# Relative-position bias rows of a fused transformer: written to a small HBM scratch and copied from there, instead of copied out of eight partitions

## The chip, the cores and the metric

One core of one Trainium2 chip runs the whole program in one launch. The metric is the device time of one execution in microseconds (us); the time before is the median of 3 runs. Instruction times in the profile are counted from the first instruction of the program; this length is called the span.

## The reference

Two layers of a first block (feed-forward, a mixer with three attention branches, feed-forward) are followed by one layer of a second block, whose attention adds a learned bias by relative position. Sequence 512, width 1024, feed-forward width 2816, float32. What the change touches is the bias:

```python
def dilated_group_attention(q, k, v, bias_tab, window, dilation):
    ...
    offset = a - c + n_prev * BLOCK
    bias = bias_tab[rel_bucket(offset * dilation)].astype(jnp.float32).transpose(2, 0, 1)
    ...
    s = jnp.einsum('brnqhd,brnkhd->brnhqk', qb, kb).astype(jnp.float32) * (Dh ** -0.5) + bias
    s = jnp.where(valid[:, None], s, NEG_INF)

def swiglu_ffn(x, g, w_gu, w_down):
    h = rms_norm(x, g)
    gate, up = jnp.split(h @ w_gu, 2, axis=-1)
    return (jax.nn.silu(gate) * up) @ w_down
```

The bias depends on the difference of two positions alone, so one row of 384 values per head (3 groups of 8 heads) holds all of it. Query i reads its own window of that row, shifted by one place from query to query.

## The kernel before

Every product is computed as three float32r matmuls (lines 172 to 174), high times high, high times low, low times high, with 128x128 of weights as the stationary side and 512 tokens as the moving side. The weights come as one stream of 550 units of 128x1024 float32 (512 KB). `w_dma` (line 133) loads unit u on the SP queue into one of three staging slots. `w_prep` (lines 141, 142) turns it into a high and a low half with one ScalarE copy and one VectorE subtraction, in a ring of five units, up to three units ahead of the one in use. A load is issued when the subtraction has freed its staging slot. One unit feeds 8 x 3 = 24 matmuls.

The program starts with the first feed-forward, `gen_ffn`. It walks over 22 chunks of 128 hidden channels: 16 weight tiles (48 matmuls) for gate and up, then `evac` (lines 261 to 263, 179, 180). Chunks 0 and 1 go together; behind them the norm's statistics are summed (line 218), turned into a reciprocal root on VectorE (lines 205 to 223) and spread over the partitions (lines 231, 232). Program order is priority: a scheduler orders each engine's instructions from it and from its own simulated times.

`bias_rows` is called once from this feed-forward. For each of the three groups it multiplies the table by one-hot rows (line 1015, in PSUM), adds the mask (line 1018, 8 partitions x 384), and issues one DMA on the GpSimd queue that writes each of the 8 rows 128 times into `dr_b` in HBM, 1.5 MB (line 1019):

```python
            if cs[0] == 2 and self.first:
                self.first = False
                self.bias_rows()
...
            nc.gpsimd.dma_start(self.dr_b[g], t[:, None, :].to_broadcast([8, 128, 384]))
```

`dr_b` is read far later, in the second block: `load_bias` reads it with a step of 383 instead of 384 from partition to partition, which gives each query its shifted window.

Of the kernel before, what the change touches and what calls it, by code (L numbers as in the profile page):

```python
# [19 lines left out]
NEG = -1.0e30  # L20
# [73 lines left out]
def const_r():  # L94
    """Stationaries: -1 where row >= column; -1 all over; identity; the strict-past mask."""
    c = np.zeros((128, 512), np.float32)
    p = np.arange(128)
    c[:, 0:128] = np.where(p[:, None] >= p[None, :], -1.0, 0.0)
    c[:, 128:256] = -1.0
    c[:, 256:384] = np.eye(128)  # L100
    c[:, 384:512] = np.where(p[:, None] < p[None, :], 0.0, NEG)
    return c
# [7 lines left out]
class Build:  # L110
# [65 lines left out]
    def split(self, hi, lo, src, scale=None):  # L176
        """hi + lo = src * scale, to float32's precision."""
        if scale is None:
            self.nc.scalar.activation(hi, src, AF.Copy)  # L179
            self.nc.vector.tensor_tensor(lo, src, hi, op=ALU.subtract)  # L180
        else:
            self.nc.scalar.activation(hi, src, AF.Copy, scale=scale)
            self.nc.vector.scalar_tensor_tensor(lo, src, scale, hi, op0=ALU.mult, op1=ALU.subtract)  # L183
# [28 lines left out]
    def stats_a(self, accs, ps, eps=1e-6, ts=range(4)):  # L212
        """Column sums of the accs into token-major rstd [128, 4]."""
        nc = self.nc
        first = None
        for i, acc in enumerate(accs):
            for t in ts:
                first = self.behind(first, nc.tensor.matmul(
                    ps[:, t:t + 1], lhsT=acc[:, 128 * t:128 * t + 128], rhs=self.f(A_C + C_ONE, 1), start=first is None,
                    stop=i == len(accs) - 1, skip_group_check=True))  # L220
        sm = self.f(A_SM, 16)
        v, a, b, y = (sm[:, i + ts[0]:i + ts[-1] + 1] for i in (4, 8, 12, 0))
        nc.vector.tensor_scalar(v, ps[:, ts[0]:ts[-1] + 1], 1.0 / D, eps, op0=ALU.mult, op1=ALU.add)
        self.rsqrt(y, v, a, b)
        return y

    def bcast(self, cols, dg, ps, out):
        """out[:, t*128 + i] = cols[i, t] on every partition."""
        nc = self.nc
        for t in range(cols.shape[-1]):  # L230
            nc.vector.tensor_scalar_mul(dg[:, 128 * t:128 * t + 128], self.f(A_C + C_ID, 128), cols[:, t:t + 1])
        nc.tensor.matmul(ps, lhsT=self.f(A_C + C_ONE, 128), rhs=dg, start=True, stop=True)
        nc.scalar.activation(out, ps, AF.Copy)
# [10 lines left out]
    def gen_ffn(self, wgu, wdn, l, done, halves=None):  # L244
# [22 lines left out]
        def up(cs):  # L267
            ps = {(c, up): self.bank(ring) for c in cs for up in (0, 1)}
            order = [(c, up, k) for c in cs for up in (0, 1) for k in range(8)]
            if len(cs) == 2:  # L270
                order.sort(key=lambda e: e[2])
            for c, up, k in order:
                self.mm3(ps[c, up], self.w(gkey(c, up, k)), self.h(k), k == 0, k == 7)
                yield
            if len(cs) == 2:
                pst = self.bank(ring)
                self.bcast(self.stats_a((self.acc,), pst), tt_flat, pst, rb)
            for c in cs:
                evac(c, ps[c, 0], ps[c, 1])
            if cs[0] == 2 and self.first:  # L280
                self.first = False
                self.bias_rows()
# [3 lines left out]
        def down(grp, cs):  # L286
# [17 lines left out]
            # the last channels a half of the tokens at a time  # L304
# [22 lines left out]
    def ffn_add(self, gain, last=None):  # L327
        """x += 0.5 * rstd * product; the second half also readies the next operand."""
        nc = self.nc

        def done(grp, m, ps, t, rb):
            x = self.x(m)
            nc.vector.tensor_tensor(t, ps, rb, op=ALU.mult)
            nc.vector.scalar_tensor_tensor(x, t, 0.5, x, op0=ALU.mult, op1=ALU.add)
            if grp == 1:
                if gain is None:
                    nc.gpsimd.dma_start(self.ap["out"][:, m, :], x)
                else:
                    self.x_done(m, gain)
        return done  # L340

    def drive(self, main, side=None):
        """Program order is priority: the side stream goes first, the main one as far as it is waited for."""
        alive = True

        def step():
            nonlocal alive
            try:
                next(main)
            except StopIteration:  # L350
                alive = False

        if side is not None:
            for tok in side:
                if isinstance(tok, str):
                    while tok not in self.flags:
                        assert alive, tok
                        step()
        while alive:
            step()  # L360

    def behind(self, first, ins):
        """A product issues behind the one that opens its bank (the first, when there is none yet)."""
# [7 lines left out]
    @contextlib.contextmanager  # L371
    def late(self, by):
        """Work that other work goes before where both are ready."""
        tc = self.tc
        p = tc.cur_priority
        tc.cur_priority = max(0, p + by)
        yield
        tc.cur_priority = p
# [7 lines left out]
    def gen_mix(self, l):  # L386
# [69 lines left out]
        # compressed branch: the rows (parity, channel) of its first product's operand  # L456
# [69 lines left out]
        # the first branch's part of the merge, in the operand's place  # L526
# [14 lines left out]
    def merged(self, m):  # L541
        """Where the merge of a chunk of channels gathers."""
        return self.mt[:, 512 * m:512 * m + 512]

    def h_tile(self, dtype=F32R):
        """The products' operand; while none is there, the merge's sums."""
        return self.hp.tile([128, 8192 if dtype == F32R else 4096], dtype, name="h", tag="h")

# [1 line left out]
    def rope(self, x, co, si, h, tmp):  # L550
        """x: [128, b, n, >= 2h], co/si: [128, b, 2h]."""
# [12 lines left out]
    def norm_heads(self, x, nh, gain, sq, sm):  # L564
        """x: [128, nh, 64] in place: rms norm over the last axis, times gain."""
# [15 lines left out]
    def one_gain(g):  # L581
        """The same gain for every head."""
# [5 lines left out]
    def tpose_dup(self, ps, src, tmp, rep=2):  # L588
        """src [128 tokens, n, d]: each [tokens, d] transposed into a column block, rep times down the partitions."""
# [8 lines left out]
    def gen_idx(self, l):  # L598
# [62 lines left out]
        # the key of the sparse branch  # L661
# [7 lines left out]
        # gates of the three branches  # L669
# [44 lines left out]
    def sb_pair(self, hp):  # L714
        """Two heads of the stick-breaking branch, key blocks from the last to the first."""
# [44 lines left out]
    def attn_pair(self, q, k, mask, n, gate, v, out, first):  # L760
        """Two heads over n keys: out[channel, token] += gated softmax times values, a head in each half of the rows."""
# [43 lines left out]
    def q2_prep(self, b, src, nh):  # L805
        """Transposed [hi; lo] queries of one block of tokens: [128, nh * 128]."""
# [28 lines left out]
    def q_prep(self, o, nh, g, sm):  # L835
        """Queries of 4 * nh heads at o: norm and rotation in place."""
# [5 lines left out]
    def gen_nsa(self, l):  # L842
# [8 lines left out]
        def prep(b):  # L851
            """Queries, and the compressed branch's numerators, transposed."""
# [152 lines left out]
    def bias_rows(self):  # L1005
        """Relative-position bias rows of every head, to DRAM."""
# [6 lines left out]
        for g in range(3):  # L1013
# [5 lines left out]
            nc.gpsimd.dma_start(self.dr_b[g], t[:, None, :].to_broadcast([8, 128, 384]))  # L1019
# [95 lines left out]
    def conv(self, c, u):  # L1115
        """Causal depthwise filter of one chunk of channels, a tap at a time in the background."""
# [26 lines left out]
    def gen_attn2(self):  # L1143
# [30 lines left out]
        def tok(g):  # L1174
            """The statistics in DRAM, [token, group, kind, head], as group g's layout has the tokens."""
# [5 lines left out]
        for hp in range(4):  # L1181
# [25 lines left out]
            # statistics of the three groups meet token by token  # L1207
# [94 lines left out]
    def gen_ln(self):  # L1302
        """Layer norm over channels of the filtered signal, silu, split for the product."""
# [34 lines left out]
    def post(self, y, next_gain, rb, ts=range(4), pool=()):  # L1338
        """x += rms_norm(y) * gain, y transposed with the gain already in it, its squares summed."""
# [85 lines left out]
    def run(self, upto=99, start=0):  # L1425
        tc, nc, ap = self.tc, self.nc, self.ap
        with tc.tile_pool(name="sb", bufs=1) as sb, tc.tile_pool(name="hp", bufs=1) as self.hp, \
# [11 lines left out]
            self.dr_b = dr.tile([3, 8, 128, 384], F32, name="dr_b")  # L1439
            self.dr_c = dr.tile([8, 128, 512], F32, name="dr_c")  # L1440
# [63 lines left out]
def tile_t(v):  # L1504
    """[..., 1024] -> [128, 8] per vector, side by side."""
# [4 lines left out]
def par_array(inp):  # L1510
    """Small parameters, one [128, PAR] array per phase."""
# [25 lines left out]
def bias_consts():  # L1537
    """Rows of one-hot buckets by position, 383 or 255 long, and what is added: 0, or NEG where no key is."""
# [46 lines left out]
```

## Time and profile before

| | |
|---|---|
| median of 3 runs | 3584.28 us |
| lowest, highest | 3582.41, 3585.07 us |
| span of the profiled execution | 3581.1 us |
| PE busy in it | 3481.8 us, 97% |
| weight stream, SP queue | 290.49 MB, 24.1% of 16 DMA engines |
| GpSimd queue | 61.76 MB, 6.8% of 16 DMA engines |

The execution that was profiled has no other time of its own than its span; the runs' median lies 3.2 us above it, and what lies around the span is taken as that. The profile names engines PE (TensorE matmul), DVE (VectorE), ACT (ScalarE), POOL (GpSimd) and SP (its DMA queue). PEclk is the share of TensorE's full clock that was granted. DMA queue q1 carries the weight stream, q0 what GpSimd issues.

### The profile page before, as it was taken

To read this page: it belongs to the slowest core of one execution; us is meant where nothing else is said; L and a number is where in the kernel's file an instruction comes from. 1 tells how busy PE (TensorE), PEld (TensorE's weight loads), DVE (VectorE), ACT (ScalarE), POOL (GpSimd) and SP (SyncE) were. 2 spreads that over 40 slices of the span, in tenths; PEclk is the share of its full clock that TensorE was granted. 3 is DMA by queue.
4 is the path that set the end of the run, shared out by engine and by line. 5 is a ranking of instruction groups with operands and counts; after the bars stand their busy time and mean duration, and the time that the engine had idled before them with its cause. 6 is when DMAs were issued, how large, how long until landed. Compare 5 with 4: busy or idle time off the path is not lost.

```text
span 3581.1 us, 43236 instructions
## 1 busy us (share of the span) xinstructions
PE 3481.8 (97%) x16884; PEld 2802.7 (78%) x16884; DVE 2001.0 (56%) x3733; ACT 1316.6 (37%) x2234; POOL 320.8 (9%) x355
## 2 busy tenths in 40 slices
PE   7899999999999999999999999999999999999997
PEld 5688888776788888888787768888877777878886
DVE  4243488566543344434876666433488988544334
ACT  3222354356332233223544464222334443443222
POOL 2000100011300010001000104000111112210002
PEclk9899999999999999999999999999999999999999
DMA  6722332331322222223322314222332224522221
GB/s 148 116 94 94 119 94 86 103 114 62 121 90 98 94 97 89 99 94 112 95 89 101 114 38 147 94 94 94 114 100 86 81 78 142 182 77 94 95 94 54
DMA packets 100814, 357.05 MB, mean 100 GB/s; under 512 B 14168, under 2 KB 16984, under 8 KB 99808
## 3 DMA queue, kind: packets, MB, share of 16 engines
q1 hardware_dynamic: 81504, 290.49, 24.1%
q0 software_dynamic: 18144, 61.76, 6.8%
q8 instruction: 132, 2.16, 0.2%
q10 hardware_dynamic: 960, 2.04, 0.2%
q14 instruction: 74, 0.61, 0.1%
HBM read 320.05 MB, written 32.08 MB: 98 GB/s over the span
## 4 chain that ended last, share of the span: by engine, by line
PE 90%; issue 3%; DMA 3%; DVE 2%; ACT 1%; POOL 1%; another core or an unknown queue 0%; DVEq 0%; ACTq 0%; POOLq 0%
PE pb L172 27%; PE pb L173 27%; PE pb L174 27%; DMA af<-wst 2%; PE pb L801 1%; PE pb L777 1%; PE pb L793 1%; PE pb L1193 1%; PE pb L737 1%; PE pb L1290 1%; PE pb L1266 1%; PE pb L595 0%; PE pb L756 0%; DMA af<-x 0%; PE pb L751 0%
## 5 line engine op out<-in xcount | busy, mean ns | idle before, releaser
L172 PE MATMUL pb<-h,ar 128*128 128x512 f32 x2848 | 1132.8, 401 | 34.6 <-ACT ar L141 16.4
L141 ACT ACTIVATE ar<-af 128x1024 fp32r<-128x1024 f32 x550 | 582.5, 1059 | 1565.1 <-PE pb L173 993.2
L174 PE MATMUL pb<-h,ar 128*128 128x512 f32 x2848 | 1140.7, 401 | 0.1
L173 PE MATMUL pb<-h,ar 128*128 128x512 f32 x2848 | 1140.1, 400 | 0.0
L142 DVE TENSOR_TENSOR ar<-af,ar 128x1024 fp32r<-128x1024 f32 x550 | 687.2, 1250 | 448.6 <-ACT ar L141 435.6
L172 PEld LDWEIGHTS pb<-h,ar 128*128 128x128 f32 x2848 | 540.8, 190 | 167.3 <-ACT ar L141 17.3
L174 PEld LDWEIGHTS pb<-h,ar 128*128 128x128 f32 x2848 | 540.6, 190 | 130.4 <-issue 3.2
L173 PEld LDWEIGHTS pb<-h,ar 128*128 128x128 f32 x2848 | 540.7, 190 | 129.0 <-issue 3.2
L173 PE MATMUL pb<-ar 128*128 128x512 f32 (+1 forms) x1254 | 484.0, 386 | 1.2 <-DVE ar L183 1.2
L174 PE MATMUL pb<-ar 128*128 128x512 f32 (+1 forms) x1254 | 483.3, 386 | 0.0
L172 PE MATMUL pb<-ar 128*128 128x512 f32 (+1 forms) x1254 | 482.4, 387 | 0.6 <-DVE af L779 0.5
L200 POOL TENSOR_TENSOR af<-af 128x512 f32<-128x512 f32 (+1 forms) x76 | 109.6, 1442 | 1857.6 <-ACT af L198 1846.5
L172 PEld LDWEIGHTS pb<-ar 128*128 128x128 f32 x1254 | 235.7, 188 | 49.8 <-DVE af L779 1.2
L173 PEld LDWEIGHTS pb<-ar 128*128 128x128 f32 x1254 | 235.8, 188 | 48.9 <-DVE ar L183 2.4
L174 PEld LDWEIGHTS pb<-ar 128*128 128x128 f32 x1254 | 235.7, 188 | 46.8
L263 DVE TENSOR_TENSOR af<-pb,af 128x512 f32<-128x512 f32 x110 | 75.7, 691 | 317.2 <-PE pb L174 316.1
L261 DVE TENSOR_TENSOR af<-pb,af 128x512 f32<-128x512 f32 x110 | 75.5, 691 | 264.4 <-PE pb L174 249.3
L1132 DVE SCALAR_TENSOR_TENSOR af<-af 128x512 f32<-128x512 f32 x240 | 179.5, 748 | 3.6
L172 PE MATMUL pb<-ar,h 128*128 128x256 f32 (+1 forms) x448 | 134.1, 299 | 0.0
L173 PE MATMUL pb<-ar,h 128*128 128x256 f32 (+1 forms) x448 | 133.2, 297 | 0.0
L174 PE MATMUL pb<-ar,h 128*128 128x256 f32 (+1 forms) x448 | 132.4, 296 | 0.0
L180 DVE TENSOR_TENSOR ar<-af,ar 128x512 fp32r<-128x512 f32 (+4 forms) x178 | 114.4, 649 | 16.3 <-ACT ar L179 15.6
(236 smaller groups left out, 3185.5 us busy)
## 6 DMA issues: line engine op xcount, KB each, us to landing
af<-wst SPq DMA_DIRECT2D x550, 512.0 KB, 3.3
dr_g<-af POOLq DMA_DIRECT2D x64, 256.0 KB, 2.3
af<-dr_g POOLq DMA_DIRECT2D x24, 512.0 KB, 4.5
dr_x<-af POOLq DMA_DIRECT2D x3, 2048.0 KB, 7.3
af<-dr_x POOLq DMA_DIRECT2D x3, 2048.0 KB, 8.7
dr_b<-af POOLq DMA_DIRECT2D x3, 1536.0 KB, 66.4
h<-dr_g POOLq DMA_DIRECT2D x16, 256.0 KB, 6.0
af<-x POOLq DMA_DIRECT2D x8, 256.0 KB, 12.4
```

What stands on the lines that cost most here:

```text
L141: self.nc.scalar.activation(self.r(o, UNIT), st, AF.Copy)
L142: self.nc.vector.tensor_tensor(self.r(o + UNIT, UNIT), st, self.r(o, UNIT), op=ALU.subtract)
L172: mm(out, lhsT=w[0], rhs=a[0], start=start, stop=False, skip_group_check=True)
L173: mm(out, lhsT=w[0], rhs=a[1], start=False, stop=False, skip_group_check=True)
L174: mm(out, lhsT=w[1], rhs=a[0], start=False, stop=stop, skip_group_check=True)
L180: self.nc.vector.tensor_tensor(lo, src, hi, op=ALU.subtract)
L200: nc.gpsimd.tensor_tensor(acc, acc, t, op=ALU.add)
L261: nc.vector.tensor_tensor(gs[i], pg, rb, op=ALU.mult)
L263: nc.vector.tensor_tensor(gs[i], pu, gs[i], op=ALU.mult)
L737: mm(z[u], lhsT=qk(2 + hp, lk)[rs[u], ks], rhs=qk(hp, lq)[rs[u], 128 * j:512], start=i == 0, stop=False, skip_group_check=True)
L777: opens = self.behind(opens, mm(ps, lhsT=q[u], rhs=k[u][l][:, 0:n], start=opens is None, stop=l == 1, skip_group_check=True))
L1132: nc.vector.scalar_tensor_tensor(a, u[:, j:j + 512], w[:, j:j + 1], a, op0=ALU.mult, op1=ALU.add)
```

## The change

The mask-added rows of a group go once to a scratch `dr_r` in HBM (8 rows, 12 KB), and a second DMA copies them 128-fold from there into `dr_b`. The call moves from behind chunk 2 to behind chunk 8 of the first feed-forward. The rest of the difference takes comments out.

```diff
-            if cs[0] == 2 and self.first:
+            if cs[0] == 8 and self.first:
                 self.first = False
                 self.bias_rows()
...
             nc.vector.tensor_tensor(t, ps[0:8, 0:384], cb[0:8, 1152 + 384 * g:1536 + 384 * g], op=ALU.add)
-            nc.gpsimd.dma_start(self.dr_b[g], t[:, None, :].to_broadcast([8, 128, 384]))
+            nc.gpsimd.dma_start(self.dr_r[g], t)
+            nc.gpsimd.dma_start(self.dr_b[g], self.dr_r[g][:, None, :].to_broadcast([8, 128, 384]))
...
             self.dr_b = dr.tile([3, 8, 128, 384], F32, name="dr_b")
+            self.dr_r = dr.tile([3, 8, 384], F32, name="dr_r")
```

How it moves instructions, at the places that matter. POOL's queue before, from the loads of x to the end of the first feed-forward (L200 adds up the squares for a norm: the first seven for this feed-forward's, the last six for the next stage's):

```order
L1450 DMA af<-x 128x512 x8
L200 ISA
L200 TENSOR_TENSOR af<-af 128x512 x5
L1019 DMA dr_b<-af 1024x1x384
L200 TENSOR_TENSOR af<-af 128x512 x2
L1019 DMA dr_b<-af 1024x1x384 x2
L200 TENSOR_TENSOR af<-af 128x512 x6
```

and now:

```order
L1452 DMA af<-x 128x512 x8
L200 ISA
L200 TENSOR_TENSOR af<-af 128x512 x7
L1019 DMA dr_r<-af 8x384 x2
L1020 DMA dr_b<-dr_r 1024x1x384
L1019 DMA dr_r<-af 8x384
L1020 DMA dr_b<-dr_r 1024x1x384 x2
L200 TENSOR_TENSOR af<-af 128x512 x6
```

The first of the large copies stood between the sums of the start-up; now all three stand behind them, each behind its small write, and the next work on POOL is that of the next stage.

On DVE, before, the first bias row stood in the start-up, while x is made ready (L240) and the first weight units are split (L142):

```order
L240 SCALAR_TENSOR_TENSOR h<-af,h 128x512 x3
L142 TENSOR_TENSOR ar<-af,ar 128x1024
L1018 TENSOR_TENSOR af<-pb_76,af 8x384
L240 SCALAR_TENSOR_TENSOR h<-af,h 128x512 x2
L142 TENSOR_TENSOR ar<-af,ar 128x1024
```

Now the three follow each other behind the evacuation of chunk 8 (L261, L263):

```order
L263 TENSOR_TENSOR af<-pb_71,af 128x512
L1018 TENSOR_TENSOR af<-pb_72,af 8x384
L142 TENSOR_TENSOR ar<-af,ar 128x1024
L1018 TENSOR_TENSOR af<-pb_73,af 8x384
L180 TENSOR_TENSOR ar<-af,ar 128x512
L1018 TENSOR_TENSOR af<-pb_74,af 8x384
L261 TENSOR_TENSOR af<-pb_75,af 128x512
```

The scheduler had pulled one row far ahead of its place in the program and the two others not; now none is pulled ahead. On PE the three small products stand behind chunk 8's last matmul:

```order
L174 MATMUL pb_71<-h,ar 128x512
L1015 MATMUL pb_72<-af 8x384
L1015 MATMUL pb_73<-af 8x384
L1015 MATMUL pb_74<-af 8x384
L172 MATMUL pb_75<-h,ar 128x512
```

SP's queue is the same, and behind chunk 8 every engine's order is as before.

## Rows read from the trace of the kernel before

**Rows 1.** The page, busy time and share of the span by engine.
```profile
PE 3481.8 (97%) x16884; PEld 2802.7 (78%) x16884; DVE 2001.0 (56%) x3733; ACT 1316.6 (37%) x2234; POOL 320.8 (9%) x355
```

**Rows 2.** Stretches of 20 us: PE, PEld, DVE, ACT, POOL busy, PEclk, DMA share, GB/s.
```profile
40.00:60.00 20.00, 5.34 (x23) 3.96 (x21) 4.13 (x14) 3.17 (x3) 0.00 (x0) 0.69 0.53 116
...
80.00:100.00 20.00, 20.00 (x87) 16.09 (x87) 4.95 (x6) 3.05 (x4) 0.00 (x0) 1.00 0.95 49
100.00:120.00 20.00, 12.33 (x53) 9.60 (x51) 0.00 (x0) 0.00 (x0) 0.00 (x0) 0.90 0.99 75
120.00:140.00 20.00, 11.14 (x29) 7.71 (x30) 4.25 (x5) 3.15 (x4) 0.00 (x0) 0.67 0.97 110
```

**Rows 3.** Timeline of PE: start us, length us, instruction, [idle before <-what ended it].
```profile
61.07 2.08 PE L232 MATMUL pb<-af 128*128 128x512 f32 x2 [15.73 <-DVE af L231]
...
64.64 0.40 PE L172 MATMUL pb<-h,ar 128*128 128x512 f32 x1
...
123.94 0.79 PE L172 MATMUL pb<-h,ar 128*128 128x512 f32 x1 [11.62 <-ACT ar L141]
...
129.57 0.39 PE L172 MATMUL pb<-h,ar 128*128 128x512 f32 x1
...
132.14 0.40 PE L174 MATMUL pb<-h,ar 128*128 128x512 f32 x1
137.37 0.79 PE L172 MATMUL pb<-h,ar 128*128 128x512 f32 x1 [4.83 <-ACT ar L141]
...
143.06 0.44 PE L172 MATMUL pb<-h,ar 128*128 128x512 f32 x1
```

**Rows 4.** Timeline of ACT: weight units being split, and what they waited for.
```profile
48.95 1.06 ACT L141 ACTIVATE ar<-af 128x1024 fp32r<-128x1024 f32 x1 [23.38 <-DMA af<-wst]
...
122.83 1.06 ACT L141 ACTIVATE ar<-af 128x1024 fp32r<-128x1024 f32 x1 [36.65 <-DMA af<-wst]
```

**Rows 5.** Timeline of POOL: the three bias copies, and the next work behind them.
```profile
22.25 1.11 POOL L1019 DMA_DIRECT2D dr_b<-af  x1
...
72.43 1.09 POOL L1019 DMA_DIRECT2D dr_b<-af  x1 [46.03 <-DVE af L1018]
75.21 1.05 POOL L1019 DMA_DIRECT2D dr_b<-af  x1 [1.70 <-DVE af L1018]
382.99 1.38 POOL L200 TENSOR_TENSOR af<-af 128x512 f32<-128x512 f32 x1 [306.72 <-ACT af L198]
```

**Rows 6.** Line 1019, the bias copies: from issue to landing.
```profile
DMA to landing us min/median/max: 33.8/66.4/66.4
```

**Rows 7.** DMA queues from 24 to 45 us: packets, MB, share of 16 engines.
```profile
q0 software_dynamic: 584, 1.07, 47.8%
q1 hardware_dynamic: 254, 0.94, 12.7%
```

**Rows 8.** DMA queues from 74 to 105 us: all that moved packets.
```profile
q0 software_dynamic: 674, 1.49, 92.4%
q8 instruction: 1, 0.02, 0.2%
```

**Rows 9.** DMA queues from 106 to 136 us.
```profile
q0 software_dynamic: 318, 1.46, 90.5%
q1 hardware_dynamic: 299, 1.09, 8.9%
```

**Rows 10.** DMA issues, whole span: count, KB each, median us from issue to landing.
```profile
af<-wst SPq DMA_DIRECT2D x550, 512.0 KB, 3.3
...
dr_x<-af POOLq DMA_DIRECT2D x3, 2048.0 KB, 7.3
af<-dr_x POOLq DMA_DIRECT2D x3, 2048.0 KB, 8.7
...
dr_s<-af POOLq DMA_DIRECT2D x16, 2.0 KB, 2.1
```

**Rows 11.** Groups from 0 to 140 us: the bias rows' products, busy us and mean ns.
```profile
L1015 PE MATMUL pb<-af 32*8 32x384 f32 x6 | 2.4, 482 | 0.0
```

## The prediction

> **What bounds the kernel now.** I read the page first, then PE in stretches of 20 us, then its timeline where it is idle, then ACT and the DMA queues in the same places. TensorE is busy for 97% of the span [rows 1], so a change to three DMAs can only gain where PE stands still. It does so in one place: between 40 and 140 us [rows 2]. The timeline shows three stops, of 15.73, 11.62 and 4.83 us [rows 3]. The second and third wait for ACT's split of a weight unit, which itself waits for the load, 36.65 us in the longest case [rows 4]. The first waits for the norm's statistics on VectorE (L231). In VectorE's order these stand behind the split of a weight unit (L142), and ACT had waited 23.38 us for that unit's load [rows 4]. So all three stops are late weights, although a load lands in 3.3 us as a rule [rows 10].
>
> The loads are late because of the bias copies. They are issued at 22.25, 72.43 and 75.21 us [rows 5] and land after 33.8, 66.4 and 66.4 us [rows 6]; the stops fall inside, or up to 5 us behind. From 24 to 45 us, with one copy under way, its queue takes 47.8% of the sixteen DMA engines, about eight of them, for 1.07 MB in 21 us, 51 GB/s [rows 7]. From 74 to 105 us two copies take 92.4% and still move only 1.49 MB in 31 us, 48 GB/s [rows 8]. Twice the engines, no more bytes: the limit lies at what they share, the eight partitions they read, not at the engines. And in those 31 us the weight queue does not appear at all [rows 8]: while copies that were queued first go on, the loads behind them don't begin. From 106 us on both queues move, the weights 1.09 MB in 30 us, 36 GB/s [rows 9]. PE needs 24 matmuls at 0.234 us (11 of them from 129.57 to 132.14 us [rows 3]) per 524 KB unit, one unit in 5.6 us, 93 GB/s.
>
> **What goes.** The stops: 15.73 + 11.62 + 4.83 = 32.2 us. Behind each of them PE runs at half clock for a while: the granted clock is 0.69, 0.90 and 0.67 in the stretches with stops and 1.00 between [rows 2]. From 123.94 to 129.57 us there are 12 matmuls in 5.63 us, where full pitch would need 2.8; from 137.37 to 143.06 again 12, in 5.69 us; from 61.07 to 64.64 us the 3.57 us are at half speed too [rows 3]. That is 2.8 + 2.9 + 1.8 = 7.5 us. Together 39.7 us can go, and no more, since outside these places PE does not stand still because of the copies.
>
> **What is added or moved, and costs nothing.** The six products of line 1015 take 2.4 us on PE in either place [rows 11]. The three sums of line 1018 stay on VectorE. Three small writes of 12 KB are new on POOL; the nearest row, 2 KB to HBM, lands in 2.1 us [rows 10], and each copy now waits for one, so some 2 to 5 us pass before the copies start. Behind the waiting instructions on POOL stands nothing until 382.99 us [rows 5], and nobody reads the bias before the second block. If that cover were gone, it would be these 5 us. SP's queue is unchanged. The nine chunks before the new place are 432 matmuls, 101 us at full pitch, so the copies fall behind the start-up's loads, into a steady weight stream.
>
> **What the copies cost in their new place** is the one open price: no row shows a copy from HBM to HBM. Each moves 1.57 MB, again on about eight engines, for its rows are still eight. From above: at the old 48 to 51 GB/s, 31 to 33 us each and 94 us in all. From the fast side: a 2048 KB write to HBM lands in 7.3 us, a read in 8.7 us [rows 10], on all sixteen. On eight, the slower of the two, scaled to 1.57 MB, is 8.7 x 2 x 0.75 = 13 us; the sum, if reading and writing don't overlap, is 16.0 x 2 x 0.75 = 24 us. The eight partitions that held the old copies back are no longer read, so I take 13 to 24 us each, 26 to 48 us in all if two fall on the same engines and the third runs beside.
>
> PE doesn't feel this. In steady state it has weights for 38 us: with no weight moving from 74 us on [rows 8], it stopped at 123.94 - 11.62 = 112.3 us [rows 3]. The first copy did harm after only 21 us (24 to 45 us) because VectorE's statistics stood behind a late unit, which is gone from the new place. Beside the old pair the weights were shut out for 31 of some 66 us, half of it; half of 48 us is 24, under 38. Afterwards they take turns with packets that are faster than the old ones. I take 0 us.
>
> [...]
>
> **The sum.** The profiled execution: 3581.1 - 39.7 = 3541.4 us of span. The median of the runs lies 3.2 us above that span, so 3544.6 us; with the small terms left out, **3545 us**. Against 3584.28 that is 1.1%.
>
> **The rivals.**
> 1. *The start-up's stop stays.* x and the tables are loaded just ahead of it, on the same engines as the weights. Then only 11.62 + 4.83 + 2.8 + 2.9 = 22.2 us go: 3562 us. Against it: ACT's wait ends at 48.95 us [rows 4], and from 24 us on it is q0 that holds half the engines at 51 GB/s [rows 7].
> 2. *The copies are faster than before, but not fast enough*, 70 us in all. Weights needed in that time: 70 x 0.093 = 6.5 MB. Delivered: none in the first 23 us, then 47 us at some 48 GB/s (36, scaled by 94 to 70), 2.3 MB; in hand 38 us, 3.5 MB. Short 0.7 MB, 8 us, and 3 us of half clock: 3556 us.
> 3. *HBM is as slow a source as the eight partitions*, 94 us in all. Needed 8.8 MB, delivered 63 us x 36 GB/s = 2.3, in hand 3.5: short 3.0 MB, 32 us, and 6 us of half clock. 38 of the 39.7 us come back: 3583 us, no change. The same reckoning gives the old pair 14 us where 16.5 were measured, so it is rough. [...]
> 4. *The other side: the eight rows are a hot spot.* All engines read the same 12 KB again and again. Below 48 GB/s in all it is slower than before; at half of that, 188 us: needed 17.5 MB, delivered 125 us x 18 GB/s = 2.3, in hand 3.5, short 11.7 MB or 126 us, and 8 us of half clock. 94 us more than before: 3679 us. For it: the old copies too were bound by what they read. Against it: no read of HBM in this trace is near so slow, the 2048 KB read moves 241 GB/s [rows 10]; but none of them reads the same bytes twice.
>
> That the change does not do what it says can't be: the order shows the copies behind chunk 8.
>
> **Chances.** Forecast 0.75, rival 1 0.07, rival 2 0.08, rival 3 0.05, rival 4 0.05. The forecast's own range is 3541 to 3551 us. From 3540 to 3560 it holds forecast and rival 2, 83%. A measurement of this kernel can tell about 0.2% (7 us) from no change. Faster by more than that are the forecast and rivals 1 and 2, 0.90; same 0.05; slower 0.05.
>
> **What would show it.** Right: no idle time of PE over 1 us between 30 and 140 us; a granted clock of 1.00 there; the first copy from scratch issued between 110 and 125 us and landing in 13 to 26 us; the weight loads delayed beside it, with PE going on. Chunks 2 to 9 at 11.2 us each. Wrong: a stop of PE some 38 us behind the first copy (rivals 2 to 4, told apart by the landing times), or a stop near 45 us (rival 1).

## The result, and the profile after

The changed kernel takes **3541.61 us** (median of 4 runs, 3540.82 to 3542.71) beside 3583.35 us (4 runs of the kernel before): ratio 0.9888, 95% interval 0.9876 to 0.9900, 41.7 us faster. Forecast were 3545 us and 39.7 us. The span fell from 3581.1 to 3540.2 us, by 40.9.

PE in stretches of 20 us of the changed kernel (PE, PEld, DVE, ACT, POOL busy, PEclk, DMA share, GB/s), beside [rows 2]:

```profile
20.00:40.00 20.00, 20.00 (x92) 16.23 (x91) 14.91 (x25) 7.64 (x10) 5.31 (x4) 1.00 0.54 170
40.00:60.00 20.00, 20.00 (x85) 15.80 (x84) 11.59 (x15) 10.71 (x14) 0.00 (x0) 1.00 0.25 80
...
100.00:120.00 20.00, 20.00 (x84) 14.65 (x83) 8.31 (x11) 4.80 (x6) 2.68 (x4) 1.00 0.31 107
120.00:140.00 20.00, 20.00 (x87) 16.09 (x86) 7.07 (x9) 5.89 (x8) 2.19 (x2) 1.00 0.81 276
140.00:160.00 20.00, 20.00 (x87) 16.05 (x87) 8.16 (x9) 5.28 (x7) 0.00 (x0) 1.00 0.38 133
```

PE is busy throughout, at the full granted clock. Where the copies run, from 118 us on, the DMA engines are at 81% and PE does not notice. Its timeline at the place of the first stop, beside [rows 3], where L232 came at 61.07 us after 15.73 us of idle time:

```profile
43.95 0.40 PE L173 MATMUL pb<-h,ar 128*128 128x512 f32 x1
44.19 1.02 PE L232 MATMUL pb<-af 128*128 128x512 f32 x2
44.65 0.80 PE L174 MATMUL pb<-h,ar 128*128 128x512 f32 x1
```

The statistics are ready when PE comes to them. ACT's splits of weight units in the start-up, beside [rows 4], where one waited 23.38 us:

```profile
24.63 1.06 ACT L141 ACTIVATE ar<-af 128x1024 fp32r<-128x1024 f32 x1 [0.17 <-DVE h L240]
30.30 1.06 ACT L141 ACTIVATE ar<-af 128x1024 fp32r<-128x1024 f32 x1 [4.60 <-DMA af<-wst]
33.65 1.06 ACT L141 ACTIVATE ar<-af 128x1024 fp32r<-128x1024 f32 x1 [2.29 <-PE pb L173]
```

One wait of 4.60 us for a load is left. From 33.65 us on ACT waits for PE to free a place in the ring, as it should. POOL's queue, beside [rows 5]:

```profile
115.94 0.54 POOL L1019 DMA_DIRECT2D dr_r<-af  x1 [90.16 <-DVE af L1018]
117.54 0.53 POOL L1019 DMA_DIRECT2D dr_r<-af  x1 [1.06 <-DVE af L1018]
118.14 1.11 POOL L1020 DMA_DIRECT2D dr_b<-dr_r  x1
119.25 0.50 POOL L1019 DMA_DIRECT2D dr_r<-af  x1
122.68 1.11 POOL L1020 DMA_DIRECT2D dr_b<-dr_r  x1 [2.93 <-DMA dr_r<-af]
132.33 1.08 POOL L1020 DMA_DIRECT2D dr_b<-dr_r  x1 [8.54 <-DMA dr_r<-af]
342.18 1.38 POOL L200 TENSOR_TENSOR af<-af 128x512 f32<-128x512 f32 x1 [208.77 <-ACT af L198]
```

Line 1020, the copies, from issue to landing, beside [rows 6]:

```profile
DMA to landing us min/median/max: 12.7/13.7/15.2
```

The DMA queues from 119 to 145 us (packets, MB, share of 16 engines), beside [rows 7 to 9]:

```profile
q0 software_dynamic: 2176, 4.76, 50.0%
q1 hardware_dynamic: 618, 2.22, 27.4%
```

A copy lands in 13.7 us instead of 33.8 to 66.4. 4.76 MB in 26 us are 183 GB/s, nearly four times the old rate, and the weights get 2.22 MB in the same time, 85 GB/s, beside a need of 93.

### The profile page after: what moved, and what is told of

The parts are those of the page before. It is cut to its first block, busy times and chain, and to the rows that moved or that the text cites. A ratio compares the mean times of both kernels' runs of the same rounds, so it can differ in the third digit from the quotient of the medians.

```text
span 3540.2 us, 43243 instructions
## 1 busy us (share of the span) xinstructions
PE 3473.6 (98%) x16884; PEld 2795.1 (79%) x16884; DVE 2002.0 (57%) x3733; ACT 1316.6 (37%) x2234; POOL 322.0 (9%) x358
## 4 chain that ended last, share of the span: by engine, by line
PE 96%; DVE 2%; ACT 1%; issue 1%; DMA 0%; POOL 0%; DVEq 0%; ACTq 0%; POOLq 0%
PE pb L172 28%; PE pb L173 28%; PE pb L174 28%; PE pb L801 2%; PE pb L793 1%; PE pb L777 1%; PE pb L1194 1%; PE pb L595 1%; PE pb L737 1%; PE pb L1291 1%; PE pb L1267 1%; PE pb L756 0%; PE pb L751 0%; PE pb L500 0%; PE pb L753 0%
## 5 line engine op out<-in xcount | busy, mean ns | idle before, releaser
L172 PE MATMUL pb<-h,ar 128*128 128x512 f32 x2848 | 1130.4, 400 | 18.0 <-ACT h L239 12.7
L142 DVE TENSOR_TENSOR ar<-af,ar 128x1024 fp32r<-128x1024 f32 x550 | 688.0, 1251 | 382.5 <-ACT ar L141 369.4
L200 POOL TENSOR_TENSOR af<-af 128x512 f32<-128x512 f32 (+1 forms) x76 | 110.2, 1450 | 1759.3 <-ACT af L198 1748.1
L263 DVE TENSOR_TENSOR af<-pb,af 128x512 f32<-128x512 f32 x110 | 75.7, 691 | 326.8 <-PE pb L174 325.9
L261 DVE TENSOR_TENSOR af<-pb,af 128x512 f32<-128x512 f32 x110 | 75.5, 691 | 278.8 <-PE pb L174 262.0
## 6 DMA issues: line engine op xcount, KB each, us to landing
dr_b<-dr_r POOLq DMA_DIRECT2D x3, 1536.0 KB, 13.7
```

The lines of the kernel that those rows point to most:

```text
L142: self.nc.vector.tensor_tensor(self.r(o + UNIT, UNIT), st, self.r(o, UNIT), op=ALU.subtract)
L172: mm(out, lhsT=w[0], rhs=a[0], start=start, stop=False, skip_group_check=True)
L200: nc.gpsimd.tensor_tensor(acc, acc, t, op=ALU.add)
L261: nc.vector.tensor_tensor(gs[i], pg, rb, op=ALU.mult)
L263: nc.vector.tensor_tensor(gs[i], pu, gs[i], op=ALU.mult)
```

## The experiments

Each is compared with 7 runs of the kernel before on the same chip: median 3581.99 us for the move alone, the source alone, the partitions four apart and the thirty-two partitions; 3582.47 us for the partitions two apart, the copies made twice and the old copies one at a time; 3582.53 us for the last. The differences shown are the lines that matter, against the changed kernel where nothing else is said.

**The move alone.** The old copy, called at the new place (against the changed kernel):

```diff
-            nc.gpsimd.dma_start(self.dr_r[g], t)
-            nc.gpsimd.dma_start(self.dr_b[g], self.dr_r[g][:, None, :].to_broadcast([8, 128, 384]))
+            nc.gpsimd.dma_start(self.dr_b[g], t[:, None, :].to_broadcast([8, 128, 384]))
```

> The move alone: called behind chunk 8, but each row still written 128-fold straight out of eight partitions, no scratch. Theory (the source's rate decides, the place only helps): three copies still move some 50 GB/s together, 94 us in all, land after 33 us or more each; the weights in hand last 38 us, so PE stops between 30 and 45 us behind the first copy, for 20 to 35 us in all with half clock behind it: 3565 to 3583 us; the stop near 45 us is gone. Rival (the place decides, the source is a trifle): no stop, 3541 to 3550 us.

Measured: 3562.11 us, ratio 0.9945 (0.9930 to 0.9960), 19.9 us faster: half of the gain, outside both ranges. The mechanism is the theory's. The last copy lands 96.5 us after its issue, as reckoned, and PE's timeline has nine stops from 45 us behind the first copy on, 15.9 us in all (the three longest):

```profile
163.71 0.50 PE L172 MATMUL pb<-ar 128*128 128x512 f32 x1 [2.39 <-ACT ar L141]
...
176.56 0.79 PE L172 MATMUL pb<-ar 128*128 128x512 f32 x1 [6.31 <-ACT ar L141]
...
199.87 0.50 PE L172 MATMUL pb<-ar 128*128 128x512 f32 x1 [4.29 <-ACT ar L141]
```

The price was too high. One reason is seen: the weights were not shut out as fully as beside the old pair. The weight queue from 118 to 150 us:

```profile
q1 hardware_dynamic: 178, 0.66, 5.5%
```

and from 150 to 214 us:

```profile
q1 hardware_dynamic: 1213, 4.41, 18.4%
```

That is 21 GB/s at first and 69 GB/s later, 5.1 MB in all, where the reckoning had 2.3.

**The source alone.** The scratch, at the old place:

```diff
-            if cs[0] == 8 and self.first:
+            if cs[0] == 2 and self.first:
```

> The source alone: scratch and copy from HBM, but called behind chunk 2 as before the change. Theory (the source's rate decides): each copy lands in 12 to 16 us, no stop of PE over 2 us, 3540 to 3546 us. Rival (the place decides: at the start-up even a short copy makes a unit late that the norm's statistics stand behind): a stop near 45 us of 5 us or more stays, 3548 to 3562 us.

Measured: 3544.44 us, ratio 0.9894 (0.9879 to 0.9908), 37.6 us faster. PE is busy for 20.00 us in every stretch from 20 to 220 us, at a clock of 1.00; the copies land in 13.2 us at the median. The theory holds: the fast source is enough even in the start-up, and what the place adds to it is within the intervals.

**Eight partitions, four apart.** Is it HBM, or that the eight partitions are neighbours? The table is repeated so that the product makes each row four times, and every fourth partition is copied 128-fold, with no scratch, behind chunk 8:

```diff
+        rep = self.f(o + 3480, 96)[0:32]
+        nc.vector.tensor_copy(rep.rearrange("p (n r) -> p n r", r=4), tab[:, :, None].to_broadcast([32, 24, 4]))
...
-            nc.gpsimd.dma_start(self.dr_r[g], t)
-            nc.gpsimd.dma_start(self.dr_b[g], self.dr_r[g][:, None, :].to_broadcast([8, 128, 384]))
+            nc.gpsimd.dma_start(self.dr_b[g], t[0:32:4][:, None, :].to_broadcast([8, 128, 384]))
```

> Called behind chunk 8, no scratch: written 128-fold straight out of eight partitions as before the change, but of partitions 0, 4, 8 to 28 instead of 0 to 7 (the product makes each row four times; a small VectorE copy of the table is added). [...] Theory B (reading so few partitions again and again is slow as such, or SBUF is a slow source): each lands after 33 us or more, stops as with the move alone, 3565 to 3583 us.

Measured: 3542.28 us, ratio 0.9889 (0.9872 to 0.9905). The copies land in 17.8, 19.7 and 29.5 us; the three run side by side here. PE does not stop, and all three are done in 30 us instead of 97, so theory B falls.

**Eight partitions, two apart.** The same with each row twice and `t[0:16:2]` (against the run with four apart):

```diff
...
-            nc.gpsimd.dma_start(self.dr_b[g], t[0:32:4][:, None, :].to_broadcast([8, 128, 384]))
+            nc.gpsimd.dma_start(self.dr_b[g], t[0:16:2][:, None, :].to_broadcast([8, 128, 384]))
```

> As the run with eight partitions four apart, but two apart (0, 2, 4 to 14). [...] Theory B (any step between the partitions frees the reads): as with four apart, all done in 30 us. Theory C (the step matters only from four on): all done in 95 us, 3562 us.

Measured: 3542.46 us, ratio 0.9889 (0.9874 to 0.9904), no stop. The copies' queue in the stretch in which the three run, for neighbours (the move alone, 117 to 214 us):

```profile
q0 software_dynamic: 2109, 4.73, 71.1%
```

for four apart (118 to 148 us):

```profile
q0 software_dynamic: 2106, 4.73, 61.1%
```

and for two apart (119 to 167 us):

```profile
q0 software_dynamic: 2111, 4.73, 67.4%
```

The landings of the three copies two apart:

```profile
DMA to landing us min/median/max: 31.3/33.8/47.5
```

Neighbours: 4.73 MB in 97 us, 49 GB/s. Two apart: 4.73 MB in 48 us, 99 GB/s. Four apart: 4.73 MB in 30 us, 158 GB/s. The same rows, the same eight entries outermost, the same destination: only the step changes, and the rate doubles with the first doubling of it. Theories B and C fall: all three copies were done in 48 us, not in 30 and not in 95. What held the old copies back, and over how many neighbours it reaches, these runs do not show. From two apart to four apart the rate rises 1.6-fold and no longer doubles; what limits it at 158 GB/s was not tested.

**Thirty-two partitions.** Each row on four neighbouring partitions, each written 32-fold, to see whether more rows take more of the engines (against the run with four apart):

```diff
...
-            nc.gpsimd.dma_start(self.dr_b[g], t[0:32:4][:, None, :].to_broadcast([8, 128, 384]))
+            nc.gpsimd.dma_start(self.dr_b[g].rearrange("h (r j) n -> (h r) j n", r=4),
+                                t[:, None, :].to_broadcast([32, 32, 384]))
```

> Called behind chunk 8, no scratch: each row stands on four neighbouring partitions, 32 in all, and each partition is written 32-fold. [...]

Measured: 3543.84 us, ratio 0.9892 (0.9877 to 0.9906). The copies land in 11.2, 17.0 and 23.7 us. From 118 to 142 us:

```profile
q0 software_dynamic: 1076, 4.61, 80.7%
```

That is 192 GB/s: hardly more than the changed kernel's 183 GB/s, out of HBM, at 50.0% of the engines, and worth nothing in the time, since PE feels neither.

**Every copy twice.** The second time into a scratch that nobody reads:

```diff
+            nc.gpsimd.dma_start(self.dr_b2[g], self.dr_r[g][:, None, :].to_broadcast([8, 128, 384]))
```

> The changed kernel with every copy made twice (the second time into a scratch that nobody reads): 9.4 MB instead of 4.7, one look at how much of the cover is left. Theory (weights take turns with packets that are short, and 38 us of weights are in hand): all six done in 45 to 60 us, no stop of PE, 3540 to 3546 us. Rival (the weights are shut out as long as copies are queued): a stop of 5 us or more some 40 us behind the first copy, 3548 to 3560 us.

Measured: 3542.73 us, ratio 0.9888 (0.9873 to 0.9903), no stop of PE. From 116 to 180 us 9.50 MB of copies and 5.77 MB of weights move; the weights get 90 GB/s, beside a need of 93. Between 105 and 190 us ACT waits for no load at all, so the cover is not near its end.

**The old copies, one at a time.** Out of partitions 0 to 7, without scratch, behind chunks 4, 8 and 12, with `bias_rows` doing one group at a time:

```diff
-            if cs[0] == 8 and self.first:
-                self.first = False
-                self.bias_rows()
+            if cs[0] in (4, 8, 12) and self.first:
+                self.bias_rows((cs[0] - 4) // 4)
+                self.first = cs[0] != 12
...
```

> The old slow copies out of partitions 0 to 7, no scratch, but one at a time: behind chunks 4, 8 and 12, some 45 us apart. Theory (a slow copy alone takes 31 to 34 us; the start-up has 21 us of weights before it is felt, the steady state 38 us): no stop, each copy lands in 33 to 36 us, 3541 to 3546 us, the whole gain without a faster source. Rival (slow packets cost the weight stream something wherever they are): 5 us or more a copy, 3556 us or more.

Measured: 3543.13 us, ratio 0.9890 (0.9874 to 0.9907): the whole gain, and no faster source. The landings of the three copies:

```profile
DMA to landing us min/median/max: 34.9/35.1/35.8
```

and two stretches of 20 us with a copy under way (columns as above):

```profile
80.00:100.00 20.00, 20.00 (x87) 16.09 (x86) 5.54 (x7) 4.70 (x6) 0.00 (x0) 1.00 0.61 108
...
120.00:140.00 20.00, 20.00 (x87) 16.05 (x87) 7.04 (x8) 4.77 (x6) 0.00 (x0) 1.00 0.62 114
```

The queues beside the second copy, from 118 to 151 us:

```profile
q0 software_dynamic: 690, 1.56, 42.9%
q1 hardware_dynamic: 609, 2.23, 18.6%
```

The weights get 68 GB/s beside one slow copy, less than the 93 that PE needs, and in this run ACT waits for a load for up to 11.3 us; the weights in hand cover it. So here a slow copy that was alone in the steady state cost nothing in the time (3543.13 us). It cost where it met another one (3562.11 us with the move alone), or the start-up (3562.66 us with the first copy early, the next run).

The packets tell the two cases apart. Alone, a packet of the slow copy takes 0.33 us of an engine's time (42.9% of sixteen engines for 33 us, 690 packets). In the old pair it is 0.68 us (92.4% for 31 us, 674 packets [rows 8]), for about as many bytes in all: the second copy added no bytes and held the other engines too. In the changed kernel it is 0.10 us (50.0% for 26 us, 2176 packets). These are estimates from the rows named.

**The first copy early.** As the last, but the first group where it was before the change, the others behind chunks 8 and 12 (against the last run):

```diff
-            if cs[0] in (4, 8, 12) and self.first:
+            if cs[0] in (2, 8, 12) and self.first:
...
```

> The old slow copies out of partitions 0 to 7, no scratch: the first where it was before the change (pulled into the start-up), the second and third alone behind chunks 8 and 12. Theory (the first copy harms because the start-up feels a late unit at once, through the norm's statistics; the other two only because they ran side by side): the stop near 45 us is back, 15 to 16 us and some 2 us of half clock, and no other: 3558 to 3561 us, about 17.5 us above the three copies spaced out. Rival (the first stop is the start-up's own loads, or the second copy's work): no stop near 45 us, 3541 to 3546 us.

Measured: 3562.66 us, ratio 0.9949 (0.9933 to 0.9966), a little above the range and 19.5 us above the spaced copies' 3543.13; in the profiled executions the spans are 3558.7 and 3541.7 us, 17.0 apart. The stop of [rows 3] is back, and alone:

```profile
61.20 2.08 PE L232 MATMUL pb<-af 128*128 128x512 f32 x2 [15.60 <-DVE af L231]
```

So the first copy in the start-up made 17 to 19.5 us of the loss. The rest, some 20 to 22 us, is left by subtraction for the second and third, which ran side by side; no run has those two alone.

## Why the prediction was right

**The bound.** That all three stops were late weights, and the weights late because of the copies, held: with the copies fast, or slow but apart, all stops and the half clock behind them are gone. Rival 1 (the start-up's own loads) fell with the source alone, which has no stop near 45 us, and with the first copy early, which has it again. What the start-up's loads leave is one wait of 4.60 us on ACT, and PE does not feel it.

For the first stop the prediction named one late unit; it was two. ACT and VectorE of the kernel before:

```profile
51.18 0.15 DVE L223 TENSOR_SCALAR af<-pb 128x4 f32<-128x4 f32 x1
55.73 1.06 ACT L141 ACTIVATE ar<-af 128x1024 fp32r<-128x1024 f32 x1 [5.72 <-DMA af<-wst]
56.82 1.23 DVE L142 TENSOR_TENSOR ar<-af,ar 128x1024 fp32r<-128x1024 f32 x1 [5.48 <-ACT ar L141]
57.96 0.16 DVE L205 TENSOR_SCALAR af<-af 128x4 int32<-128x4 int32 x1
```

Behind the unit that ACT had waited 23.38 us for, only the first step of the statistics (L223) went. The others (from L205 on) stood behind a second unit, whose load took 5.72 us more. The cause is the same, late weights.

**What goes.** Predicted 39.7 us; the span fell by 40.9. The page of the changed kernel, beside [rows 1]:

```profile
PE 3473.6 (98%) x16884; PEld 2795.1 (79%) x16884; DVE 2002.0 (57%) x3733; ACT 1316.6 (37%) x2234; POOL 322.0 (9%) x358
```

PE's idle time (span less busy time) fell from 99.3 to 66.6 us, by 32.7, where 32.2 were forecast for the stops; its busy time fell by 8.2 us, where 7.5 were forecast for the half clock. So both terms came out, not only their sum. The 1.2 us between are less than the spread of the kernel before (3579.31 to 3585.07 us). That PE stood still "in one place" was too narrow: some 67 us of its idle time lay elsewhere, and the copies had no part in them. Of the 3.4 us by which 3545 us was too high, the span makes 1.2; the rest is the 3.2 us put on top of it. In the execution profiled now the time is 1.8 us above the span (3541.96 and 3540.2), and between 1.7 and 1.9 us in every run here whose span is known; the 3.2 us also held the distance of one execution from the median.

**What was costed at nothing.** Line 1015 takes 2.1 us in its new place, where 2.4 were counted in either. The small writes landed in 1.7, 4.9 and 12.8 us where 2 to 5 was said. The second was issued 0.6 us ahead of the first copy and the third 1.1 us behind its issue; POOL stood 2.93 and 8.54 us for them, and the third copy was issued only as the first had landed. The cover named for it, nothing behind them on POOL (now until 342.18 us), held.

**The copies' price.** Predicted 13 to 24 us each and 26 to 48 us in all, from the 2048 KB rows to and from HBM, scaled to half the engines. No run shows that a copy out of HBM takes twice as long on half the engines; that was the author's estimate. Measured: 12.7 to 15.2 us at 50.0% of the engines, and 27 us from the first issue at 118.14 to the last landing (132.33 plus 12.7). The fast end was right, the one that counts only the slower of reading and writing. The waits for the small writes had a part in the sum: the third copy was issued 14.2 us behind the first. Reading the same eight rows again and again did not make HBM slow here (rival 4), and HBM was not as slow as the partitions (rival 3): 183 GB/s beside 48 [rows 8].

**The share of the engines** was about half, as the prediction took it: 50.0% for the copies of eight rows, beside 47.8% for one old copy [rows 7]. It had no price: with thirty-two rows and 80.7% the time is no better, 3543.84 us. That run reads SBUF; whether copies out of HBM would be shorter on more engines, no run shows. What the eight partitions share was left open; the two runs with a step show that the step counts: 49 GB/s for neighbours, 99 two apart, 158 four apart.

**Where the reckoning was off** is the price of slow copies in rivals 2 and 3. Rival 3, three copies of 94 us in all, was put at 3583 us; the move alone is that case and took 3562. One term that failed is what the weights get meanwhile: nothing for a third of the time and 36 GB/s after it, from [rows 8, 9], against 21 and then 69 GB/s. The copies held 92.4% of the engines in those rows, and 92.9% from 118 to 150 us in the move alone; why three copies shut the weights out less than two, these runs don't tell. Nor does the reckoning come out with that term put right: 8.9 MB needed in 96 us, 5.1 delivered and 3.5 in hand leave 0.3 MB or 3 to 4 us short, and PE stood 15.9 us. So two errors stood against each other, and a sum of bytes was not enough to price these copies. Why, no run shows.

**What each part was worth.** Source alone 37.6 us, move alone 19.9, both 41.7; the old copies merely apart 39.3. The parts don't add up, because both cures remove the stop in the start-up. The fast source removes the later ones too; the move leaves three slow copies side by side, which cost some 20 us. A short copy nowhere uses up the weights in hand, and in the steady stream neither does a long one that is alone. None of the versions tried is faster than the changed kernel by more than the intervals.

## What to carry to other kernels

A DMA that nobody waits for can still set the time, here by 41.7 us, by delaying the stream that everybody waits for: look at the landing times of that stream while it runs. Its price here was what it kept from the stream against the work that the stream had in hand, and not its length alone. One slow copy of 35 us cost nothing in the steady state and 17 to 19.5 us in the start-up, and two together some 20 to 22 us. Copies out of partitions two apart ran for 48 us, longer than the 38 us of weights in hand, and cost nothing, because the weights got 4.02 MB, 84 GB/s, beside them. Rows on eight neighbouring partitions were copied at 49 GB/s, two apart at 99 and four apart at 158; either step did as much for the time (3542.46 and 3542.28 us) as going through HBM (3541.61 us), with no wait for a scratch.

## What the runs showed that was not expected

Copying out of HBM what was just written there, 8 rows 128 times over, ran at 183 GB/s beside a weight stream of 85 GB/s: for this size, a row that is read again and again is no hot spot. A write of 12 KB took 12.8 us to land when it was issued 1.1 us behind a copy of 1.5 MB on the same queue, against 1.7 us for the quickest. And twice the copies, 9.50 MB, cost PE as little as the 4.76.
